# Weight sums by transfers that add in place, a changed order of the seven products, and transposes dealt out between matmuls

## The chip, the cores and the metric

The kernel runs on one core of a Trainium2 chip. The time is device microseconds of one execution; the time given for a kernel is the median of its runs. Engines are named as in the profile: PE (TensorE), DVE (VectorE), ACT (ScalarE), POOL (GpSimd), SP (the queue that issues most transfers).

## The reference, cut to what matters

Two layers work on x of 1024 rows by 1024 columns. Layer 0 mixes rows by differential attention, layer 1 by retention. Each layer norms its input, applies a scale and shift, projects, mixes, projects out and adds the normed result:

```python
h = rms_norm(x) * (1 + scale) + shift          # per layer
q, k, v, g = split(einsum("bsd,de->bse", h, w_in))   # layer 1: widths 1024, 1024, 2048, 2048
y = silu(g) * head_rms_norm(mix(q, k, v))      # layer 1: retention, 4 heads, 256 and 512 wide
x = x + gate * rms_norm(einsum("bse,ed->bsd", y, w_out))
```

What the change touches is the step from layer 0 to layer 1 and layer 1's product h·w_in, with h 1024x1024 and w_in 1024x6144, both f32.

## The kernel before

**Precision.** Matmuls take f16. Each f32 operand is split into a high and a low f16 part, and three matmuls (high·high, high·low, low·high) stand for one f32 product. The split of a weight tile is `prepare`: an ACT copy (L810, high part) and a DVE operation (L811, low part).

**Layer 1's input products.** The 6144 columns of w_in are taken as 12 blocks (`Columns`; per head c_q for q and k, c_v for v, c_g for the gate), each of two groups of 256 columns. A block of w_in has four quarters B11, B12, B21, B22 of 512x256 f32 (512 KB), and h has quarters too (A11 and so on, and their differences S1, M2, N3, N4). A block is computed with seven products of quarters instead of eight, listed with the chain (a PSUM bank) that each is added to:

```python
PRODUCTS = (("x", "A11", "B11"), ("y", "A12", "B21"), ("x", "M2", "T2"), ("z", "S1", "T1"),
            ("x", "N3", "T3"), ("x", "A22", "T4"), ("z", "N4", "B22"))
```

The sums are T1 = B11 + B12, T3 = B12 + B22, T2 = B22 + T1, T4 = B21 + T2. In `prepare` they are four DVE additions per block (L798), three ahead of the split of T2 and one ahead of T4. T2 takes B22's buffer, so B22 is loaded a second time for the last product: five loads of 512 KB per block, all issued by SP (L773). Raw quarters have 4 buffers (`raws1`), split weights 5 (`ws1`); a product's weight is prepared three products ahead (`AHEAD`) and loaded further ahead (`LOADS`).

`product` (L837) runs the matmuls of one product: 256 columns each for q and k, for which h is the moving operand or the weight by column group, and 512 columns for v and g. It then copies a chain's value aside on ACT (L851), or adds kept values on DVE (L846). A chain that starts anew needs a PSUM bank whose former value has been read.

**The turn from layer 0 to layer 1.** Row tiles of 128 rows leave layer 0 by `out0(t)`: the out-projection (`outproj`, 48 matmuls of 512 columns, L574), its norm and the residual (`residual`, L586 on ACT, L589 and L591 on DVE), the store of x, and the norm of the next layer (L304 on ACT, L146 and L149 on POOL, L629 on DVE), which gives `xns[t]`. `out0_hT(j)` turns row tiles 2j and 2j+1 into the quarters of h: 16 transposes of 128x128 f32 on PE in 4 groups of 4 (L651), after each group two scaled copies on ACT (L653) that empty its PSUM bank, and after two groups the sums and splits of h's quarters (L658 to L668 on DVE and ACT). The order of these steps is a string that ends in `... o5 y7 o6 h2 o7`: the 16 transposes of pair 2 stand between the projections of row tiles 6 and 7. The 16 transposes of pair 3 stand in the first block of layer 1, in one piece, after product 2 of the second group of rows (`(n, m) == (2, 1)`); the other half of that block (g = 1) needs them.

**What sets the order.** From `o6` on, PE runs in the order in which the code is written; the other engines' order is set by a scheduler when the kernel is built. Every engine works through its own queue in order: an instruction that waits holds all behind it. At the very end, 16 tiles of the last out-projection's weight (`wo1`) are put where older tiles come free; tile 3 takes a buffer of v ("vr").

Of the kernel before, what the change touches and what calls it, by code (L numbers as in the profile page):

```python
# [20 lines left out]
F16 = mybir.dt.float16  # L21
# [5 lines left out]
P = 128  # L27
# [60 lines left out]
def trunk(ctx: ExitStack, tc: tile.TileContext, a: dict, out: bass.AP):  # L88
# [476 lines left out]
            nc.vector.scalar_tensor_tensor(out=y[t][:, e], in0=o[:, i * P : (i + 1) * P], scalar=f[:, i : i + 1], in1=y[t][:, e], op0=ALU.mult, op1=ALU.mult)  # L565


    def outproj(yT, wo):
        res = []
        for n in range(2):  # L570
            ps = mm()
            for k in range(NK):
                for yi, wi in ((0, 0), (0, 1), (1, 0)):
                    nc.tensor.matmul(  # L574
                        ps, yT(yi, k), wo[k // 4][:, k % 4, wi, n * 512 : (n + 1) * 512],
                        start=(k == 0 and yi == 0 and wi == 0), stop=(k == NK - 1 and yi == 1),
                    )
            res.append(ps)
        return res
# [40 lines left out]
    def out0(t):  # L620

        xt = xres[t // 2][:, t % 2, :]
        ps = outproj(yTs[t], wts["o"])
        x1 = ys.tile([P, D], F32, name="x1", tag=f"y{t}")
        _, add = residual(ps, x1, gps[0], xt, xt)
        add(slice(0, D))
        nc.gpsimd.dma_start(out=x1_d[:, t, :], in_=xt)
        r = row_rsqrt(xt, D, 1.0, NORM_EPS)
        nc.vector.tensor_scalar(out=x1, in0=xt, scalar1=r, scalar2=None, op0=ALU.mult)  # L629
        xns[t] = x1  # L630

    def out0_hT(j):

        if j == 0:
            hA.extend(big.tile([P, 2, 2, 2, 512], F16, name="hA", tag="sb", bufs=3) for _ in range(2))
            hB.append(big.tile([P, 4, 2, 512], F16, name="hB", tag="sb", bufs=3))
            hS.extend(hts.tile([P, 2, 2, 2, 512], F16, name="hS", tag=f"h{k}") for k in range(4))
        n = slice(j * P, (j + 1) * P)
        for kh in range(2):

            pa, ta, ba = (early, "qs", 2) if j == 0 else (ys, f"y{2 * j - 2 + kh}", 1)
            pb, tb, bb = (early, "ks", 2) if j < 2 else (ys, f"y{2 * j - 4 + kh}", 1)
            t = pa.tile([P, 4, 2, P], F32, name="hq", tag=ta, bufs=ba)
            t2 = pb.tile([P, 4, 2, P], F32, name="hq2", tag=tb, bufs=bb)
            for i in range(2):
                ps = sc()
                for kk in range(2):
                    k = 2 * kh + kk + 4 * i
                    for b in range(2):
                        c = (2 * kk + b) * P  # L650
                        nc.tensor.transpose(out=ps[:, c : c + P], in_=xns[2 * j + b][:, k * P : (k + 1) * P], identity=ident)  # L651
                    m = mods[1, k]
                    nc.scalar.activation(  # L653
                        out=t[:, 2 * i : 2 * i + 2, kk], in_=ps[:, 2 * kk * P : 2 * (kk + 1) * P].rearrange("p (b e) -> p b e", b=2),
                        func=AF.Identity, scale=m[:, 1:2], bias=m[:, 0:1],
                    )
            for i in range(2):
                nc.vector.tensor_tensor(out=t2[:, i], in0=t[:, 1], in1=t[:, 3 * i], op=ALU.subtract)  # L658
            nc.vector.tensor_tensor(out=t2[:, 2], in0=t[:, 0], in1=t2[:, 1], op=ALU.subtract)
            nc.vector.tensor_tensor(out=t2[:, 3], in0=t[:, 2], in1=t2[:, 2], op=ALU.subtract)  # L660
            for src, dst, sign in (
                (t[:, 0:4:3], lambda b: hA[kh][:, :, :, b, n].rearrange("p a k e -> p (a k) e"), -1.0),
                (t[:, 2], lambda b: hB[0][:, 2 * kh : 2 * kh + 2, b, n], 1.0),
                (t2[:, 0:2].rearrange("p a k e -> p (a k) e"), lambda b: hS[2 * kh][:, :, :, b, n].rearrange("p a k e -> p (a k) e"), 1.0),
                (t2[:, 2:4].rearrange("p a k e -> p (a k) e"), lambda b: hS[2 * kh + 1][:, :, :, b, n].rearrange("p a k e -> p (a k) e"), 1.0),
            ):
                nc.scalar.activation(out=dst(0), in_=src, func=AF.Copy, scale=sign)
                nc.vector.scalar_tensor_tensor(out=dst(1), in0=src, scalar=sign, in1=dst(0), op0=ALU.mult, op1=ALU.subtract)  # L668

    def load_wo():  # L670
        wts["o"] = load_wout(a["da_w_out"][0], gsub)
# [51 lines left out]
    for h in range(6):  # L723
# [13 lines left out]
        "f": lambda t: flush(),  # L737
        "y": out0_yT,
        "o": out0,
        "h": out0_hT,  # L740
    }
    order = (
        "a0 q1 q2 a1 q0 a2 q3 b0 b1 v5 b2 v4 a3 b3 f0 y0 y1 v7 y2 v6 a4 b4 a5 y3 w0 o0 "
        "o1 b5 a6 a7 b6 y4 o2 b7 f0 y5 o3 h0 o4 y6 h1 o5 y7 o6 h2 o7"
    )
    for c in order.split():
        if c == "o6":
# [22 lines left out]
    def raw_block(src):  # L770
# [4 lines left out]


    PRODUCTS = (
        ("x", "A11", "B11"), ("y", "A12", "B21"), ("x", "M2", "T2"), ("z", "S1", "T1"),
        ("x", "N3", "T3"), ("x", "A22", "T4"), ("z", "N4", "B22"),
    )  # L780

    class Columns:
# [6 lines left out]

        def load(self, n):  # L790

            for b in {0: ("B11",), 1: ("B21", "B12"), 2: ("B22",)}.get(n, ()):
                self.raw[b] = raw_block(self.src(int(b[1]) - 1, int(b[2]) - 1))

        def prepare(self, n):

            r = self.raw
            add = lambda o, x: nc.vector.tensor_tensor(out=r[o], in0=r[o], in1=r[x], op=ALU.add)  # L798
            name = PRODUCTS[n][2]
            if name == "T2":  # L800
                add("B11", "B12")
                add("B12", "B22")
                add("B22", "B11")
                r["T1"], r["T3"], r["T2"] = r["B11"], r["B12"], r["B22"]
            elif name == "T4":
                add("B21", "T2")
                r["T4"] = r["B21"]
                r["B22"] = raw_block(self.src(1, 1))
            w = self.place[n]() if n in self.place else ws1.tile([P, 4, 2, 256], F16, name="w1", tag="w1")
            nc.scalar.activation(out=w[:, :, 0, :], in_=r[name], func=AF.Copy, scale=SW)  # L810
            nc.vector.scalar_tensor_tensor(out=w[:, :, 1, :], in0=r[name], scalar=SW, in1=w[:, :, 0, :], op0=ALU.mult, op1=ALU.subtract)  # L811
            self.w[n] = w

    class Quarters:
# [10 lines left out]
        def product(self, n, new):  # L825
# [20 lines left out]
                nc.vector.tensor_tensor(out=dst, in0=shape(src), in1=dst, op=op)  # L846
                return dst

            if n in (0, 2, 4):
                self.kept[n] = self.hold(n)  # L850
                nc.scalar.activation(out=self.kept[n][0], in_=self.kept[n][1](src), func=AF.Copy)  # L851
            if n == 1:
                self.done("11", add(0, src, ALU.subtract), 1.0)
            elif n == 4:
                self.done("22", add(4, self.acc["z"][:, 0:width], ALU.add), 1.0)
            elif n == 5:
                self.done("21", src, -1.0)
            elif n == 6:
                self.done("12", add(2, src, ALU.add), 1.0)

    def bank_for(u):
        return lambda chain: mm() if chain == "x" or u == 0 else tr()
# [19 lines left out]
    def four_tiles(cols, u, c):  # L882

        parts = [(slice(i * 256, (i + 1) * 256), None, slice((2 * u + i) * P, (2 * u + i + 1) * P)) for i in range(2)]
        two = lambda x: x.rearrange("p (b e) -> p b e", b=2)
        at = lambda q: c[:, (q[0] == "2") : 4 : 2, (q[1] == "2") * 256 : (q[1] == "2") * 256 + 256]

        def done(q, src, sign):
            if q == "21":
                nc.scalar.activation(out=at(q), in_=two(src), func=AF.Copy, scale=sign)  # L890

        return Quarters(cols, parts, lambda n: (at({0: "11", 2: "12", 4: "22"}[n]), two), done)

    steps1 = []

    def retain(h):

# [12 lines left out]
        if h == 0:  # L910
            for g in range(2):
                us = {}
                for n in range(7):
                    for m in range(2):
                        def step(n=n, m=m, g=g, us=us):
                            if n == 0 and m == 0 and g == 0:
                                begin()
                            if n == 0:
                                us[m] = queries_keys(h, st["qT"], st["kT"], c_q, m, slice(g * 256, (g + 1) * 256))
                            us[m].product(n, bank_for(m))  # L920
                            if g == 0 and (n, m) == (2, 1):
                                out0_hT(3)
                        steps1.append((c_q, n, step))
        else:
            us = {}
# [182 lines left out]

    wanted = list(dict.fromkeys((cols, n) for cols, n, _ in steps1))
    AHEAD, LOADS = 3, 6  # L1110
    ready = loaded = 0
    for cols, n, step in steps1:
        at = wanted.index((cols, n))
        while ready < min(at + AHEAD + 1, len(wanted)):
            while loaded < min(ready + LOADS - AHEAD, len(wanted)):
                wanted[loaded][0].load(wanted[loaded][1])
                loaded += 1
            wanted[ready][0].prepare(wanted[ready][1])
            ready += 1
        step()  # L1120


    w_out1 = a["ret_w_out"][0]
    wo1 = {}
    for n in range(2):
        for h in range(RET_HEADS):
# [1 line left out]
            if i < 3:  # L1128
                t = big.tile([P, 4, 2, 512], F16, name="wo1", tag="sb", bufs=3)
            elif i == 3:  # L1130
                t = ret2().tile([P, 4, 2, 512], F16, name="wo1", tag="vr", bufs=2)
            else:
                t = hts.tile([P, 4, 2, 512], F16, name="wo1", tag=f"h{i - 4}")
            for j in range(2):
# [88 lines left out]
```

## Time and profile before

| | |
|---|---|
| median of 3 runs | 1379.69 us (1378.15 to 1382.76) |
| the profiled execution's own time | 1381.89 us |
| its span | 1379.8 us |
| mean granted PE clock | 0.987 |
| stages by the trace | layer 0 to about 640 us, layer 1's blocks to about 1200 us, last projection to the end |

The profile is one execution. A median of busy shares hides the stages, so the trace is read by stretches: busy time of each engine, and the clock that PE was granted as a share of full speed.

### The profile page before, as it was taken

Reading aid. Unit: us, or ns where it says so; the run is one execution under the profiler, and the core shown is the slowest. Engines: PE = TensorE matmul, PEld = TensorE weight load, DVE = VectorE, ACT = ScalarE, POOL = GpSimd, SP = SyncE. Lnnn points to the kernel's source line nnn. Section 1 sums busy time; section 2 is a strip of 40 time slices with the busy share of each in tenths; the row PEclk is TensorE's granted clock in tenths of the full one; section 3 lists DMA queues with packets and bytes.
Section 4 is the critical chain, followed back from the end, with each engine's and each line's share of the span. In section 5 each row is a group of like instructions: output and inputs, shape, how many; then the busy total and the mean of one; then the engine's idle time right before and its main releaser. Section 6 shows DMA issues by size and latency. Waiting matters only on the chain.

```text
span 1379.8 us, 21360 instructions
## 1 busy us (share of the span) xinstructions
PE 1291.8 (94%) x8285; PEld 775.2 (56%) x8285; DVE 948.4 (69%) x1830; ACT 669.3 (49%) x1298; POOL 146.7 (11%) x254
## 2 busy tenths in 40 slices
PE   3899999999999998878999999999999999989998
PEld 2444455455445544435886658765876586634443
DVE  4866996997887786695559865986598658742011
ACT  4854544654555565565445644564456445621000
POOL 2000110111101121221001200120011001100000
PEclk9999999999999999988999999999999999999999
DMA  9723544566352356542321234233323443365330
GB/s 299 242 79 71 133 103 100 144 153 138 100 141 56 89 122 157 136 133 93 75 79 62 94 100 107 62 102 93 106 62 95 116 115 108 73 179 130 92 92 31
DMA packets 249462, 153.94 MB, mean 112 GB/s; under 512 B 147864, under 2 KB 238160, under 8 KB 249360
## 3 DMA queue, kind: packets, MB, share of 16 engines
q1 hardware_dynamic: 246192, 141.29, 39.2%
q0 software_dynamic: 3168, 11.28, 2.6%
q8 instruction: 65, 1.06, 0.3%
q14 instruction: 37, 0.30, 0.1%
HBM read 102.21 MB, written 14.68 MB: 85 GB/s over the span
## 4 chain that ended last, share of the span: by engine, by line
PE 42%; DVE 5%; ACT 5%; DMA 2%; POOL 1%; issue 1%; SPq 0%; POOLq 0%; DVEq 0%; ACTq 0%
PE ps_mm L837 20%; PE ps_av L1170 6%; PE ps_mm L1170 5%; PE ps_tr L837 5%; PE ps_sc L1019 2%; PE ps_av L1042 1%; PE ps_av L1049 1%; DMA raw1o<-in_ret_w_out 1%; PE ps_mm L574 1%; DMA raw<-in_ada_w 1%; ACT junk L304 1%; ACT sg L1060 1%; POOL rs L149 1%; POOL rs L146 1%; DVE w L811 1%
## 5 line engine op out<-in xcount | busy, mean ns | idle before, releaser
L343 PE MATMUL ps_mm<-w,hT 128*128 128x512 f16 x768 | 176.6, 380 | 0.0
L837 PEld LDWEIGHTS <-hS 128*128 128x128 f16 x1536 | 149.6, 98 | 20.5
L331 PE MATMUL ps_mm<-hT,w 128*128 128x512 f16 x624 | 142.2, 379 | 0.0
L811 DVE SCALAR_TENSOR_TENSOR w<-raw,w 128x1024 f16<-128x1024 f32 x82 | 99.9, 1220 | 56.8 <-ACT w L810 56.8
L837 PE MATMUL ps_mm<-w,hS 128*128 128x256 f16 x1152 | 131.6, 273 | 0.0
L523 ACT ACTIVATE sb<-sb,mx 128x128 f32<-128x128 f32 (+7 forms) x128 | 98.2, 768 | 65.2 <-DVE mx L516 64.7
L343 PEld LDWEIGHTS <-hT 128*128 128x128 f16 x768 | 74.5, 98 | 82.9 <-issue 0.8
L810 ACT ACTIVATE w<-raw 128x1024 f16<-128x1024 f32 x82 | 85.8, 1049 | 53.9 <-issue 33.7
L837 PEld LDWEIGHTS <-w 128*128 128x128 f16 x744 | 73.7, 99 | 64.5 <-issue 1.6
L516 DVE CUSTOM_DVE_ANT_0 sb<-ps_sc,table 128x512 f32<-128x512 f32 (+3 forms) x128 | 73.3, 585 | 36.5 <-PE ps_sc L513 28.7
L331 PEld LDWEIGHTS <-w 128*128 128x128 f16 x624 | 60.1, 98 | 67.4
L574 PE MATMUL ps_mm<-w_o,yT 128*128 128x512 f16 x384 | 92.7, 389 | 0.0
L837 PE MATMUL ps_mm<-w,hA 128*128 128x256 f16 x768 | 87.8, 273 | 0.0
L837 PEld LDWEIGHTS <-hA 128*128 128x128 f16 x768 | 74.8, 98 | 10.0
L1170 PEld LDWEIGHTS <-yT 128*128 128x128 f16 x480 | 46.9, 98 | 56.7
L178 DVE SCALAR_TENSOR_TENSOR acc<-raw,cond,acc 128x256 f32<-128x256 f32 x140 | 65.6, 480 | 10.7 <-DMA raw<-in_ada_w 9.2
L534 ACT ACTIVATE sb<-sb 128x896 f16<-128x896 f32 (+6 forms) x64 | 43.3, 678 | 55.4 <-DVE sb L531 55.3
L546 PEld LDWEIGHTS <-dT 128*128 128x128 f16 x864 | 53.7, 99 | 28.5 <-DMA dT<-sb 20.1
L512 PE MATMUL ps_sc<-ks,qs 128*128 128x512 f16 (+3 forms) x192 | 62.1, 330 | 6.9 <-DVE mx L516 6.7
L837 PE MATMUL ps_mm<-hS,w 128*128 128x512 f16 (+1 forms) x336 | 63.3, 346 | 0.0
L513 PE MATMUL ps_sc<-kl,qs 128*128 128x512 f16 (+3 forms) x192 | 62.0, 329 | 0.0
L574 PEld LDWEIGHTS <-yT 128*128 128x128 f16 x384 | 38.1, 100 | 41.8 <-issue 3.8
(205 smaller groups left out, 2290.9 us busy)
## 6 DMA issues: line engine op xcount, KB each, us to landing
raw<-in_ret_w_in SPq DMA_DIRECT2D x60, 512.0 KB, 3.7
raw<-in_ada_w SPq DMA_DIRECT2D x40, 512.0 KB, 6.4
raw<-in_da_w_in SPq DMA_DIRECT2D x16, 1024.0 KB, 6.0
raw1o<-in_ret_w_out SPq DMA_DIRECT2D x16, 512.0 KB, 4.6
y_d<-y SPq DMA_DIRECT2D x24, 256.0 KB, 2.2
x<-in_x SPq DMA_DIRECT2D x8, 512.0 KB, 7.6
raw<-in_ada_w SPq DMA_DIRECT2D x4, 1024.0 KB, 5.3
raw_o<-in_da_w_out SPq DMA_DIRECT2D x4, 1024.0 KB, 5.0
```

The source lines that it names most:

```text
L178: nc.vector.scalar_tensor_tensor(out=acc, in0=parts[k], scalar=cond[:, k : k + 1], in1=acc, op0=ALU.mult, op1=ALU.add)
L331: nc.tensor.matmul(ps, w[:, k, wi, lo : lo + P], hT[k][g][:, xi, :], start=(k == 0 and wi == 0 and xi == 0), stop=(k == NK - 1 and wi == 1),)
L343: nc.tensor.matmul(ps, hT[k][g][:, xi, j * P : (j + 1) * P], w[:, k, wi, :], start=(k == 0 and wi == 0 and xi == 0), stop=(k == NK - 1 and ...
L512: nc.tensor.matmul(ps[c][:, 0:n], qs[:, c, q], ks[:, c, k], start=True, stop=False)
L513: nc.tensor.matmul(ps[c][:, 0:n], qs[:, c, q], kl[c][:, k], start=False, stop=True)
L516: nc.vector.tensor_tensor_reduce(out=sb[:, c, k], in0=ps[c][:, 0:n], in1=table[:, S - L + lo : S - L + lo + n], scale=-es, scalar=(3.0e38 ...
L523: nc.scalar.activation(out=sb[:, c, 0:L], in_=sb[:, c, 0:L], func=AF.Exp, scale=-1.0, bias=mx[:, m0 + c : m0 + c + 1], accum_out=z[:, 4 * ...
L574: nc.tensor.matmul(ps, yT(yi, k), wo[k // 4][:, k % 4, wi, n * 512 : (n + 1) * 512], start=(k == 0 and yi == 0 and wi == 0), stop=(k == NK ...
L810: nc.scalar.activation(out=w[:, :, 0, :], in_=r[name], func=AF.Copy, scale=SW)
L811: nc.vector.scalar_tensor_tensor(out=w[:, :, 1, :], in0=r[name], scalar=SW, in1=w[:, :, 0, :], op0=ALU.mult, op1=ALU.subtract)
L837: nc.tensor.matmul(ps[:, pc], l, r, start=(first and i == 0 and k == 0 and wi == 0 and xi == 0), stop=(k == 3 and wi == 1), skip_group_che ...
L1170: nc.tensor.matmul(pso[t, n], yT1[t][2 * (k // 8) + yi][:, k % 8, :], wo1[k // 4, n][:, k % 4, wi, :], start=(k == 0 and yi == 0 and wi == ...
```

## The change

**Sums.** The four DVE additions per block (48 in all) go. In their place POOL issues four transfers per block that add to what lies in the destination: B11 += B12 and B12 += B22, both with the source in DRAM, give T1 and T3 in place; T1 += B22 from the loaded tile gives T2 in T1's own buffer; B21 += T2 gives T4. They are written in a new function `sums`, called one product ahead of `prepare`. B22 keeps its own buffer, so its second load goes: 4 loads by SP in place of 5.

**Order of products.** T2 now overwrites T1, so the product with T1 (chain z) comes third and that with T2 (chain x) fourth. B22 is loaded with product 3, and the value kept from product 2 is kept from product 3.

**Transposes.** `out0_hT` becomes a generator that stops after each group of four transposes. `h2` goes from the order; during `o7`, four transposes of pair 2 stand ahead of every 12 matmuls. Those of pair 3 are dealt out four at a time after steps (2,1), (3,0), (3,1) and (4,0) of the first half block.

**A buffer.** Tile 3 of the last weight takes the buffer "kN" of the pool `ret` instead of "vr".

```diff
...
-    def outproj(yT, wo):
+    def outproj(yT, wo, between=iter(())):
...
             for k in range(NK):
+                if k % 4 == 0:
+                    next(between, None)
                 for yi, wi in ((0, 0), (0, 1), (1, 0)):
...
-        ps = outproj(yTs[t], wts["o"])
+        ps = outproj(yTs[t], wts["o"], out0_hT(2) if t == 7 else iter(()))
...
+                if i == 0:
+                    yield
...
+            yield
...
-        "o1 b5 a6 a7 b6 y4 o2 b7 f0 y5 o3 h0 o4 y6 h1 o5 y7 o6 h2 o7"
+        "o1 b5 a6 a7 b6 y4 o2 b7 f0 y5 o3 h0 o4 y6 h1 o5 y7 o6 o7"
...
-        ("x", "A11", "B11"), ("y", "A12", "B21"), ("x", "M2", "T2"), ("z", "S1", "T1"),
+        ("x", "A11", "B11"), ("y", "A12", "B21"), ("z", "S1", "T1"), ("x", "M2", "T2"),
...
-            for b in {0: ("B11",), 1: ("B21", "B12"), 2: ("B22",)}.get(n, ()):
+            for b in {0: ("B11",), 1: ("B21", "B12"), 3: ("B22",)}.get(n, ()):
...
+        def sums(self, n):
+
+            r = self.raw
+            add = lambda o, x: nc.gpsimd.dma_start(out=r[o], in_=x, accum_op=ALU.add)
+            rows = lambda i, j: self.src(i, j).rearrange("(k p) e -> p k e", p=P)
+            if n == 2:
+                add("B11", rows(0, 1))
+                add("B12", rows(1, 1))
+                r["T1"] = r["T2"] = r["B11"]
+                r["T3"] = r["B12"]
+            elif n == 3:
+                add("T2", r["B22"])
+            elif n == 5:
+                add("B21", r["T2"])
+                r["T4"] = r["B21"]
+
         def prepare(self, n):
...
-            add = lambda o, x: nc.vector.tensor_tensor(out=r[o], in0=r[o], in1=r[x], op=ALU.add)
...
-            if name == "T2":
-                add("B11", "B12")
-                add("B12", "B22")
-                add("B22", "B11")
-                r["T1"], r["T3"], r["T2"] = r["B11"], r["B12"], r["B22"]
-            elif name == "T4":
-                add("B21", "T2")
-                r["T4"] = r["B21"]
-                r["B22"] = raw_block(self.src(1, 1))
...
-            if n in (0, 2, 4):
+            if n in (0, 3, 4):
...
-                            if g == 0 and (n, m) == (2, 1):
-                                out0_hT(3)
+                            if g == 0 and (n, m) >= (2, 1):
+                                if not last_hT:
+                                    last_hT.append(out0_hT(3))
+                                next(last_hT[0], None)
...
+            while summed <= ready:
+                wanted[summed][0].sums(wanted[summed][1])
+                summed += 1
             wanted[ready][0].prepare(wanted[ready][1])
             ready += 1
         step()
+        while summed < min(at + AHEAD + 2, loaded):
+            wanted[summed][0].sums(wanted[summed][1])
+            summed += 1
...
-                t = ret2().tile([P, 4, 2, 512], F16, name="wo1", tag="vr", bufs=2)
+                t = ret.tile([P, 4, 2, 512], F16, name="wo1", tag="kN", bufs=1)
...
```

**PE between row tiles 6 and 7.** These are PE's rows at the last matmuls of `o6` and the first transposes of pair 2 (`ps_sc` is the bank of a group, `x1` the normed row tiles 4 and 5), before:

```order
L574 LDWEIGHTS yT_5811
L574 MATMUL ps_mm_5968<-w_o_5056,yT_5811 128x512
L651 MATMUL ps_sc_6012<-ident_90,x1_5789 128x128
L651 MATMUL ps_sc_6012<-ident_90,x1_5919 128x128
L651 MATMUL ps_sc_6012<-ident_90,x1_5789 128x128
L651 MATMUL ps_sc_6012<-ident_90,x1_5919 128x128
L651 MATMUL ps_sc_6019<-ident_90,x1_5789 128x128
```

and of the change, where a group of four is followed by matmuls of row tile 7:

```order
L576 LDWEIGHTS yT_5811
L576 MATMUL ps_mm_5968<-w_o_5056,yT_5811 128x512
L653 MATMUL ps_sc_6013<-ident_90,x1_5789 128x128
L653 MATMUL ps_sc_6013<-ident_90,x1_5919 128x128
L653 MATMUL ps_sc_6013<-ident_90,x1_5789 128x128
L653 MATMUL ps_sc_6013<-ident_90,x1_5919 128x128
L576 LDWEIGHTS yT_5939
L576 MATMUL ps_mm_6010<-w_o_5047,yT_5939 128x512
```

The second group now comes 12 matmuls (24 rows with their weight loads) behind the first, in another bank.

**ACT in the same stretch.** The names are raw buffers of the first block: in the kernel before, raw1_6152 is T2 (in B22's buffer), 6146 is T1, 6150 is T3; `hq` are the scaled copies that empty a group of transposes. Before:

```order
L810 ACTIVATE w1_6163<-raw1_6152 128x4x256
L810 ACTIVATE w1_6166<-raw1_6146 128x4x256
L586 ACTIVATE junk_117,ss_5994<-ps_mm_5968 128x512
L653 ACTIVATE hq_6010<-ps_sc_6012,mod1_0_1426 128x2x128
L810 ACTIVATE w1_6203<-raw1_6150 128x4x256
L653 ACTIVATE hq_6010<-ps_sc_6012,mod1_1_1684 128x2x128
L653 ACTIVATE hq_6010<-ps_sc_6019,mod1_4_2689 128x2x128
L653 ACTIVATE hq_6010<-ps_sc_6019,mod1_5_2947 128x2x128
```

and in the change, where 6146 is first T1, then T2:

```order
L821 ACTIVATE w1_6162<-raw1_6146 128x4x256
L588 ACTIVATE junk_117,ss_5994<-ps_mm_5968 128x512
L655 ACTIVATE hq_6011<-ps_sc_6013,mod1_0_1426 128x2x128
L655 ACTIVATE hq_6011<-ps_sc_6013,mod1_1_1684 128x2x128
L821 ACTIVATE w1_6166<-raw1_6146 128x4x256
L304 ACTIVATE junk_117,ss_6004<-xres_5806 128x1024
L655 ACTIVATE hq_6011<-ps_sc_6032,mod1_4_2689 128x2x128
L821 ACTIVATE w1_6203<-raw1_6150 128x4x256
L655 ACTIVATE hq_6011<-ps_sc_6032,mod1_5_2947 128x2x128
```

T1's split comes first and T2's behind the first group's copies; each now stands in the queue ahead of copies of a later group.

**POOL in the same stretch.** `rs` are norm factors of row tiles, `x1_d` the store of x; raw1_6155 is B22 and 6148 is B21. Before:

```order
L627 DMA x1_d_101<-xres_5393 128x1024
L146 TENSOR_SCALAR rs_5932<-ss_5930 128x1
L149 TENSOR_TENSOR rs_5932<-rs_5932,negh_99 128x1
L148 TENSOR_SCALAR rs_5999<-ss_5994 128x1
L149 TENSOR_TENSOR rs_5999<-rs_5999,negh_99 128x1
L627 DMA x1_d_101<-xres_5806 128x1024
```

and in the change:

```order
L629 DMA x1_d_101<-xres_5393 128x1024
L146 TENSOR_SCALAR rs_5932<-ss_5930 128x1
L803 DMA raw1_6146<-in_ret_w_in 128x4x256
L149 TENSOR_TENSOR rs_5932<-rs_5932,negh_99 128x1
L803 DMA raw1_6146<-raw1_6155 128x1024
L148 TENSOR_SCALAR rs_5999<-ss_5994 128x1
L149 TENSOR_TENSOR rs_5999<-rs_5999,negh_99 128x1
L803 DMA raw1_6148<-raw1_6146 128x1024
L629 DMA x1_d_101<-xres_5806 128x1024
```

Three adding transfers have come between the norm factors and the stores of the last row tiles.

## Rows read from the trace of the kernel before

**Rows 1.** The page's first part: busy time, share of the span, instructions.

```profile
PE 1291.8 (94%) x8285; PEld 775.2 (56%) x8285; DVE 948.4 (69%) x1830; ACT 669.3 (49%) x1298; POOL 146.7 (11%) x254
```

**Rows 2.** Windows by stage: window, length, busy time and count by engine, clock, DMA share, GB/s.

```profile
core 0: us, PE busy (x) PEld busy (x) DVE busy (x) ACT busy (x) POOL busy (x), PEclk, DMA share, GB/s
...
600.00:700.00 100.00, 86.26 (x622) 63.75 (x620) 63.52 (x100) 49.20 (x96) 10.48 (x18) 0.90 0.33 94
700.00:1200.00 500.00, 491.96 (x3660) 351.03 (x3658) 372.54 (x522) 256.34 (x416) 44.70 (x67) 1.00 0.31 90
```

**Rows 3.** Windows of the turn, and of one later half block.

```profile
600.00:611.40 11.40, 11.40 (x55) 5.22 (x53) 10.30 (x14) 5.05 (x9) 3.05 (x5) 1.00 0.36 93
611.40:623.20 11.80, 4.08 (x17) 2.63 (x16) 10.83 (x15) 9.71 (x18) 3.20 (x5) 0.60 0.54 177
623.20:635.60 12.40, 12.40 (x50) 5.23 (x48) 5.07 (x11) 3.33 (x7) 0.00 (x0) 0.83 0.00 1
635.60:643.50 7.90, 7.90 (x74) 6.99 (x72) 4.22 (x6) 4.45 (x11) 4.23 (x8) 1.00 0.43 158
643.50:651.50 8.00, 3.38 (x20) 2.20 (x18) 6.22 (x13) 6.38 (x13) 0.00 (x0) 0.78 0.50 160
651.50:663.60 12.10, 12.10 (x98) 10.26 (x97) 6.56 (x16) 5.43 (x12) 0.00 (x0) 0.87 0.01 1
...
786.20:822.40 36.20, 36.20 (x169) 16.43 (x168) 26.34 (x33) 17.22 (x27) 2.38 (x4) 1.00 0.36 113
```

**Rows 4.** Waits in 600 to 660 us: engine, line, releaser: total, times, longest.

```profile
PE ps_sc L651 <- ACT hq L653: 12.3, 8, 3.6
```

**Rows 5.** Timeline of the turn: start, length, engine, line, operation [idle before, releaser].

```profile
604.19 2.35 DVE L811 SCALAR_TENSOR_TENSOR w<-raw,w 128x1024 f16<-128x1024 f32 x2
...
605.62 1.01 POOL L146 TENSOR_SCALAR rs<-ss 128x1 f32<-128x1 f32 x1 [0.43 <-ACT junk L304]
...
612.23 2.00 ACT L810 ACTIVATE w<-raw 128x1024 f16<-128x1024 f32 x2 [5.12 <-DVE raw L798]
...
615.31 1.12 PE L651 MATMUL ps_sc<-ident,x 128*128 128x128 f32 x4 [3.61 <-ACT hq L653]
...
619.33 1.05 ACT L304 ACTIVATE junk<-xres 128x1024 f16<-128x1024 f32 x1
...
622.77 0.69 PE L651 MATMUL ps_sc<-ident,x 128*128 128x128 f32 x2 [2.69 <-ACT hq L653]
...
641.25 0.75 DVE L629 TENSOR_SCALAR x<-xres,rs 128x1024 f32<-128x1024 f32 x1 [2.24 <-POOL rs L149]
...
645.12 0.66 PE L651 MATMUL ps_sc<-ident,x 128*128 128x128 f32 x4 [1.18 <-ACT hq L653]
```

**Rows 6.** Groups by line over the whole span: busy time, mean ns, idle before.

```profile
L811 DVE SCALAR_TENSOR_TENSOR w<-raw,w 128x1024 f16<-128x1024 f32 x82 | 99.9, 1220 | 56.8 <-ACT w L810 56.8
...
L810 ACT ACTIVATE w<-raw 128x1024 f16<-128x1024 f32 x82 | 85.8, 1049 | 53.9 <-issue 33.7 <-PE ps_tr L837 12.1 <-DVE raw L798 7.0
...
L798 DVE TENSOR_TENSOR raw<-raw,raw 128x1024 f32<-128x1024 f32 x48 | 58.7, 1222 | 1.1
...
L653 ACT ACTIVATE hq<-ps_sc,mod 128x256 f32<-128x256 f32 x32 | 16.9, 560 | 4.2 <-PE ps_sc L651 3.9
...
L627 POOL DMA_DIRECT2D x_d<-xres x8 | 4.9, 616 | 15.4 <-DVE xres L591 15.2 <-issue 0.2
```

**Rows 7.** DMA issues: operation, count, KB each, median us from issue to landing.

```profile
raw<-in_ret_w_in SPq DMA_DIRECT2D x60, 512.0 KB, 3.7
...
x_d<-xres POOLq DMA_DIRECT2D x8, 512.0 KB, 3.7
...
gp<-in_post_gain POOLq DMA_DIRECT2D x2, 512.0 KB, 4.7
```

**Rows 8.** Timeline: two evictions of product chains and what waits for one.

```profile
674.29 1.47 PE L837 MATMUL ps_tr<-hS,w 128*128 128x256 f16 x12 [1.40 <-DVE held L846]
...
691.62 0.68 DVE L846 TENSOR_TENSOR sg<-ps_mm,sg 128x512 f32<-128x512 f32 x1
```

**Rows 9.** PE's waits in 960 to 1220 us.

```profile
PE ps_sc L1019 <- DVE a L1002: 2.7, 3, 1.9
...
PE ps_mm L1170 <- DVE wo L1141: 1.7, 2, 1.5
```

More of the change, by code (lines that the diff above doesn't have):

```diff
@@ L739, in trunk @@
         "o": out0,
-        "h": out0_hT,
+        "h": lambda j: list(out0_hT(j)),
     }
@@ L858, in product @@
             elif n == 6:
-                self.done("12", add(2, src, ALU.add), 1.0)
+                self.done("12", add(3, src, ALU.add), 1.0)
     def bank_for(u):
@@ L890, in done @@
                 nc.scalar.activation(out=at(q), in_=two(src), func=AF.Copy, scale=sign)
-        return Quarters(cols, parts, lambda n: (at({0: "11", 2: "12", 4: "22"}[n]), two), done)
+        return Quarters(cols, parts, lambda n: (at({0: "11", 3: "12", 4: "22"}[n]), two), done)
     steps1 = []
+    last_hT = []
     def retain(h):
@@ L1110, in trunk @@
     AHEAD, LOADS = 3, 6
-    ready = loaded = 0
+    ready = loaded = summed = 0
     for cols, n, step in steps1:
```

## The prediction

> **What bounds the kernel now.** I read the page's first part, then busy time by stage, then the stage with the most idle PE finely: its windows, PE's waits, the timeline. PE is busy 94% of the span and DVE 69% [rows 1], but the stages differ. From 700 to 1200 us PE works 491.96 of 500 us at clock 1.00 [rows 2]: all idle time there is 8.0 us, so the DVE additions inside it (48 in the kernel, 58.7 us together [rows 6]) are hidden, and taking them away gives next to nothing. The room is in the turn between the layers: from 600 to 700 us PE works 86.26 us, and the granted clock is 0.90 [rows 2].
>
> The turn's windows show two holes. In 611.4 to 623.2 PE works 4.08 of 11.8 us at 0.60; the 48 matmuls of row tile 7 behind it take 12.4 us at 0.83. In 643.5 to 651.5 it works 3.38 of 8.0 us at 0.78, and the next 12.1 us run at 0.87 [rows 3]. Both holes are the 16 transposes of a pair in one piece: PE waits for ACT to empty the banks with L653, 8 waits, 12.3 us [rows 4]. The reader should see how: four transposes take 0.66 us undisturbed, and the waits ahead of them are 3.61 us (behind ACT's splits of T2 and T1, which waited 5.12 us for DVE's additions), 2.69 and 1.18 us [rows 5].
>
> **What a transfer that adds costs.** The trace has none, and this is the main unknown; call D its time from issue to landing. Below: a plain transfer of the same 512 KB lands 3.7 us after its issue, from SP's queue and from POOL's; the slowest median of that size on POOL's queue is 4.7 [rows 7]. An add reads two operands and writes one; if it moves at half the speed throughout, D is twice 3.7, 7.4, at the far end twice 4.7, 9.4. I take 5.6, midway between 3.7 and 7.4, since only the moving part of the 3.7 should double, and keep 3.7 and 9.4 for the range. Writing out a plain 512 KB store takes POOL 0.62 us [rows 6]; for 1 KB rows, of which there are four times as many, I allow 1.2 (an estimate). The Trainium skill ("Collectives: The Full Stack", Part 3, "Why 7× under link rate") says that the add inside a transfer costs nothing by itself, but the second source read goes through the same ring and halves the rate. That is at most 7.4 here; no run so far shows it.
>
> **The first hole, with D.** B11's add can be issued when its two splits are done and POOL has written the norm factor ahead of it: DVE's splits of B11 and B21 run from 604.19 for 2.35 us, POOL's L146 from 605.62 for 1.01 us [rows 5], so 606.6. T1 lands at 606.6 + D; its splits (1.05 on ACT, 1.22 on DVE [rows 6]) and a semaphore's 0.1 let T2's add start at 609.0 + D, which lands at 609.0 + 2D. ACT's queue now has T2's split behind the first group's copies and ahead of the norm's square (L304) and the second group's copies, so ACT stands still until then. Behind it lie 1.05 (T2), 1.25 (L304, 1.05 + 0.2), 0.56, 1.05 (T3) and 0.56 [rows 5, 6]: the second group's bank is empty at 613.5 + 2D, and the fourth group of transposes can start 0.3 later (the sets of four transposes use two banks). By PE's own work the fourth group is due at 611.3 + 3 x (0.7 + 2.6) = 621.2 (12 matmuls of 512 columns at full clock take 2.6, a quarter of some 10.4). With D = 5.6 it starts at 625.0 instead, 3.8 late; adding its 0.7, the last 2.6 and 1.5 for stretches at less than full clock, row tile 7's projection ends at 629.8 instead of 635.6 [rows 3]: **-5.7 us**.
>
> **The second hole.** The normed row tile 7 was ready 6.4 us after its projection's end (635.60 by the window, L629 from 641.25 for 0.75 [rows 3, 5]). In the change the splits of the last group of pair 2 and of T4 fall into that stretch, and I allow two splits on ACT and 0.5 for them (2.6 us): ready at 629.8 + 9.0 = 638.8. The 7.9 us of products ahead of the first group [rows 3] end at 637.7, so PE waits 1.1, and the first four transposes start near 639 instead of 643.5 (-4.5). From there to the second half of the block lie 16 transposes (4 x 0.7), the remaining eight products (12.1 us at clock 0.87 [rows 3], so 10.5 at full clock), and 2.3 that I allow for waits between the groups (twice the wait of 1.18 [rows 5]): 15.6 us instead of 20.1 (8.0 and 12.1 [rows 3]), another **-4.5**. The second half starts at 654.6 instead of 663.6: **-9.0** with the first hole's gain in it.
>
> **Behind the turn.** In the first v block T1's split waits for its add's landing (+1.5) and T2's (+1.0) while the 1.40 us wait of 674.29 [rows 8], which stood behind DVE's additions, goes: +1.1. For the later 10 blocks: a half block of v or g takes some 36 us [rows 3], T1's add is issued a product ahead, and its buffer's use lies over two products behind; T2's landing has room up to D of some 9 to 11. ACT stands still D - 3 us per block, with nothing due soon behind it. POOL is busy 44.70 of 500 us [rows 2]; four adds a block put some 4 us on it and hold norm factors of the heads by up to D; those are needed a tile later.
>
> Chain y is now followed at once by z, which may want y's bank. An eviction starts 0.2 to 0.3 us after its product and takes 0.68 [rows 8]; where DVE is busy with other work, 1 us is lost now and then, **+1** in all. Against it, DVE has 58.7 us less [rows 6], of which PE's waits for DVE in the later blocks can profit: 2.7 us for L1002 in 960 to 1220 us [rows 9] and as much again in the blocks before, of which I count **-3**. The last weight tile's new buffer comes free earlier: PE waits 1.7 us for it [rows 9]; **-1**. The SP loads that go (12 of 512 KB) lie in a stage with a DMA share of 0.31 [rows 2] and give nothing.
>
> The sum: -9.0 + 1.1 + 1 - 3 - 1 = -10.9 us against the profiled execution's 1381.9, so 1371.0; its own time lies 2.2 above the runs' median, so the median becomes 1369.
>
> **Rivals.** *Waits on ACT eat the gain.* From D = 5.6 on, each us of D costs 4: two in the first hole, where two adds follow each other, and two in the first v block. If D is 7.4, 7.2 of the 10.9 go: profile 1378, median 1376. For it speaks that nothing in the trace shows an add; against it, that the 3.7 holds a start that should not double. *Adds too slow: slower than before.* The sum is zero at D = 8.3. At D = 9.4 the turn gives 15.2 back, and from about D = 9 on each of 11 later blocks loses time where T2 is late, some 0.3 each: +7, median 1387; at D = 12, with 1.2 us for each block, about 1408. A way to it is that POOL writes a transfer's list of rows slowly while DVE works: the 3.7 and 4.7 of POOL's stores, with DVE busy 69% of the time [rows 1, 7], speak against it. The Trainium skill ("SBUF — State Buffer", the trap headed "DVE blocks DMA") says that transfers issued by POOL can starve while DVE runs an operation in its two-port mode, since their descriptors can't be written; those two landings show no such thing, but neither has 1 KB rows.
>
> *z behind y stalls.* If z waits in each of 12 blocks for y's eviction, 0.7 us each [rows 8], 8.4 go and the median is 1378.
>
> *Adds as quick as plain loads.* D = 3.7: the fourth group starts when it is due, so the first hole gives 5.4 more, the first v block 2.5 more, and row tile 7's matmuls run at full clock (12.4 us at 0.83 [rows 3], so 2.1 less): -21, median 1359. That the change does not do what it says, the holes staying, would need the transposes to wait for something else; the rows of PE and ACT show no other releaser than L653 [rows 4].
>
> **How the numbers follow.** The forecast (D from 4.6 to 6.9) has 0.53, ACT's waits 0.17, slow adds 0.20, z behind y 0.05, quick adds 0.05. The predicted time is the forecast's, 1369, with 1362 to 1376 of its own. The range goes from the value at D = 3.7 to that at 9.4, 1359 to 1387; beyond it lie half of the slow adds and half of the quick ones, and small tails of the rest. A measurement of this kernel can tell about 0.3% (4.1 us) from no change. Faster by more (below 1375.6): the forecast but 0.02, quick adds, and 0.06 of ACT's waits, 0.62. Slower (above 1383.8): slow adds, and 0.01 of ACT's waits, 0.21. The rest, 0.17.
>
> **What would show it.** In the profile after: the landing time of the accumulating transfers (5 to 6.5 us); no transposes in one piece; row tile 7's matmuls between them, at a granted clock over 0.83; L821 of T2 on ACT waiting some 5 us in the first block; the second half of the first block starting near 655; PE's idle time in 700 to 1200 us still about 8 us. The forecast is wrong if the adds land after more than 8 us, if PE waits for splits of T2 or T4 in each block, or if PE's busy time rises.

## The result and the profile after

The changed kernel takes 1395.16 us (median of 4 runs, 1394.05 to 1396.99) against 1380.28: a ratio of 1.0108, 95% interval 1.0087 to 1.013. It is slower by 1%, and the forecast was faster by 0.8%.

The page and the windows by stage (columns as in [rows 2]) after:

```profile
PE 1293.7 (93%) x8285; PEld 774.6 (56%) x8285; DVE 892.5 (64%) x1782; ACT 670.5 (48%) x1298; POOL 193.8 (14%) x302
```

```profile
600.00:700.00 100.00, 83.85 (x621) 61.75 (x620) 54.99 (x94) 48.41 (x95) 18.09 (x26) 0.97 0.53 119
700.00:1200.00 500.00, 482.92 (x3577) 343.26 (x3575) 315.28 (x465) 246.27 (x398) 81.62 (x105) 1.00 0.54 119
```

DVE has 56 us less to do than in [rows 1], and PE's own work is nearly the same. But the stage that had 8.0 us of idle PE [rows 2] now has 17.1. The DMA issues, as in [rows 7]:

```profile
raw<-in_ret_w_in SPq DMA_DIRECT2D x48, 512.0 KB, 4.5
...
raw<-in_ret_w_in POOLq DMA_DIRECT2D x24, 512.0 KB, 6.4
raw<-raw POOLq DMA_DIRECT2D x24, 512.0 KB, 4.6
```

The transfers that add land after 6.4 us (from DRAM, 1 KB rows) and 4.6 us (tile to tile): the mean of the two is 5.5, and the forecast had assumed 5.6 for both. So the main unknown was right in the mean, and the sign of the forecast wrong.

To see where the time went, each trace is cut at three starts: PE's first transpose of pair 2, the first product of the first v block, and the last projection's first matmul that adds a product of `yT` to `ps_av`. "Turn" lies between the first two, "later" between the next two, "end" behind. One profiled execution each, us; the median is that of the runs, and the ratio goes by the runs of the kernel before on the same chip (medians 1379.1 to 1380.8), with its 95% interval. For e2 both leave out one run of 3857.22 us, far above its other three:

| kernel | median | ratio to before | turn | later | end |
|---|---|---|---|---|---|
| before | 1380.28 | | 72.1 | 547.5 | 148.9 |
| changed | 1395.16 | 1.0108 (1.0087-1.0130) | 71.8 | 559.2 | 149.1 |
| e1 transposes dealt out alone | 1374.14 | 0.9965 (0.9951-0.9978) | 67.1 | 546.1 | 148.9 |
| e2 changed, transposes in one piece | 1398.75 | 1.0140 (1.0119-1.0160) | 79.0 | 559.8 | 149.1 |
| e3 changed, sums by DVE | 1381.97 | 1.0014 (1.0002-1.0026) | 69.3 | 548.8 | 149.2 |
| e4 changed, T2 and T4 by DVE | 1381.35 | 1.0010 (0.9997-1.0023) | 68.6 | 549.6 | 149.1 |
| e5 = e1 with the new order | 1381.01 | 1.0006 (0.9997-1.0016) | 73.3 | 546.2 | 148.9 |
| e6 changed, T2 in B22's buffer | 1395.25 | 1.0102 (1.0078-1.0127) | 73.0 | 562.7 | 148.9 |
| e7 changed, T2 by DVE | 1385.25 | 1.0041 (1.0025-1.0058) | 69.0 | 553.7 | 149.1 |
| e8 = e1 with the new buffer | 1374.10 | 0.9963 (0.9951-0.9975) | 66.1 | 546.5 | 148.9 |
| e10 = e1, copies behind four transposes | **1360.97** | 0.9866 (0.9845-0.9887) | 56.5 | 545.6 | 148.9 |
| e11 before, copies behind four transposes | 1366.11 | 0.9896 (0.9875-0.9918) | 60.7 | 547.1 | 150.5 |
| e12 changed, T2 split after T3 | 1385.85 | 1.0041 (1.0026-1.0056) | 72.9 | 550.2 | 149.1 |
| e13 changed, copies behind four transposes | 1387.24 | 1.0054 (1.0038-1.0070) | 63.7 | 562.9 | 149.1 |
| e14 changed, T4 by DVE | 1402.60 | 1.0171 (1.0153-1.0189) | 71.9 | 565.4 | 149.1 |

So the loss lies in "later" (+11.7), and the turn gave 0.3 where 9.0 was forecast. The spans of the two profiles differ by 12.5 us, the medians by 14.9; the profiles account for the 12.5.

**Where "later" loses.** PE's waits after, 700 to 1200 us (columns as in [rows 4]):

```profile
PE ps_sc L1033 <- DVE a L1016: 12.2, 14, 2.2
PE ps_tr L252 <- DVE sg L857: 3.3, 3, 1.2
PE ps_sc L1033 <- DVE y L980: 1.6, 1, 1.6
```

L1033 is the state's matmul of the retention steps; before, the same matmul (L1019) waited 4.6 us in that stretch:

```profile
PE ps_sc L1019 <- DVE a L1002: 4.4, 6, 1.9
...
PE ps_sc L1019 <- DVE y L966: 0.2, 1, 0.2
```

These waits grew by 9.2 us, most of the 11.7. Part of the rest is clock: behind the longest of them (2.19 us, ended at 1174.30) the granted clock from 1175 to 1185 us is 0.86. The timeline around one of these waits, after:

```profile
853.34 0.88 POOL L803 DMA_DIRECT2D raw<-raw  x1 [9.10 <-DVE w L822]
...
857.87 1.06 ACT L821 ACTIVATE w<-raw 128x1024 f16<-128x1024 f32 x1 [1.79 <-DMA raw<-raw]
...
858.84 0.40 ACT L1017 ACTIVATE aT<-a 128x256 f16<-128x256 f32 x1
...
861.50 0.68 DVE L857 TENSOR_TENSOR sg<-ps_mm,sg 128x512 f32<-128x512 f32 x1
...
862.22 1.91 ACT L970 ACTIVATE vr<-sg 128x2048 f16<-128x2048 f32 x1 [0.96 <-DVE sg L857]
...
864.16 2.29 DVE L971 SCALAR_TENSOR_TENSOR vr<-sg,vr 128x2048 f16<-128x2048 f32 x1 [1.98 <-ACT vr L970]
...
868.95 0.28 DVE L1016 TENSOR_TENSOR a<-ps_sc,dec 128x128 f32<-128x128 f32 x1
...
869.28 1.46 PE L1033 MATMUL ps_sc<-y,kN 128*128 128x512 f16 x6 [0.74 <-DVE a L1016]
```

Read it downwards. T2's add is issued at 853.34; ACT comes to T2's split and stands 1.79 us for the landing. Behind it in ACT's queue waits the copy of the scores (L1017), and so in turn DVE's eviction (L857) and the splits of v; they follow late, and L1016, which empties the scores' bank, ends at 869.23. PE's L1033 needs that bank and waited 0.74 us. Before, the same place of the same head shows no wait:

```profile
856.22 0.42 ACT L1003 ACTIVATE aT<-a 128x256 f16<-128x256 f32 x1 [0.74 <-DVE a L1002]
...
861.78 2.29 DVE L957 SCALAR_TENSOR_TENSOR vr<-sg,vr 128x2048 f16<-128x2048 f32 x1
...
865.54 2.81 PE L1019 MATMUL ps_sc<-y,kN 128*128 128x512 f16 x12
```

DVE's split of v (L957) began 0.81 us ahead of PE's next scores at 862.59 then, and just behind them (864.13) now (L971). That this chain starts with ACT's wait is a reading of one place; e12 and e7 below test it.

**Why the turn gave so little.** From 600 to 700 us PE waits 10.1 us for copies of transposes (12.3 before [rows 4]), but 6.0 us for evictions of products in three places, where it waited 1.4 before [rows 8]. Two of the three, after:

```profile
672.21 1.06 ACT L821 ACTIVATE w<-raw 128x1024 f16<-128x1024 f32 x1 [4.33 <-DMA raw<-in_ret_w_in]
...
673.59 2.78 PE L848 MATMUL ps_mm<-hS,w 128*128 128x256 f16 x24 [1.96 <-ACT held L862]
...
680.89 1.06 ACT L821 ACTIVATE w<-raw 128x1024 f16<-128x1024 f32 x1 [4.04 <-DMA raw<-raw]
...
683.92 5.40 PE L848 MATMUL ps_mm<-w,hA 128*128 128x256 f16 x48 [2.31 <-DVE qT L889]
```

The splits of T1 and T2 of the first v block stand in ACT's queue, 4.33 and 4.04 us long, for their adds to land. Behind them in the queue stand copies of the block in work (L862 and L888), and PE waits for them, the second time by way of DVE's L889.

### The profile page after: what moved, and what is told of

Its sections match the earlier page's. It is cut to its first block, busy times and chain, and to the rows that moved or that the text cites. A ratio compares the mean times of both kernels' runs of the same rounds, so it can differ in the third digit from the quotient of the medians.

```text
span 1392.3 us, 21410 instructions
## 1 busy us (share of the span) xinstructions
PE 1293.7 (93%) x8285; PEld 774.6 (56%) x8285; DVE 892.5 (64%) x1782; ACT 670.5 (48%) x1298; POOL 193.8 (14%) x302
## 4 chain that ended last, share of the span: by engine, by line
PE 29%; DMA 6%; DVE 6%; ACT 4%; issue 3%; SPq 2%; POOL 2%; POOLq 0%; DVEq 0%; ACTq 0%
PE ps_mm L848 13%; PE ps_av L1190 5%; PE ps_mm L1190 5%; DMA raw<-in_ret_w_in 3%; PE ps_tr L848 2%; DMA raw<-raw 2%; SPq L956 1%; PE ps_sc L1033 1%; DVE w L822 1%; PE ps_av L1063 1%; DMA raw1o<-in_ret_w_out 1%; PE ps_av L1056 1%; DVE sg L857 1%; ACT sg L1074 1%; DVE y L1069 1%
## 5 line engine op out<-in xcount | busy, mean ns | idle before, releaser
L516 DVE CUSTOM_DVE_ANT_0 sb<-ps_sc,table 128x512 f32<-128x512 f32 (+3 forms) x128 | 73.3, 585 | 36.3 <-PE ps_sc L513 30.0
L848 PEld LDWEIGHTS <-hA 128*128 128x128 f16 x768 | 74.8, 98 | 12.5 <-issue 2.5
```

Source lines behind the costliest of these rows:

```text
L516: nc.vector.tensor_tensor_reduce(out=sb[:, c, k], in0=ps[c][:, 0:n], in1=table[:, S - L + lo : S - L + lo + n], scale=-es, scalar=(3.0e38 ...
L848: nc.tensor.matmul(ps[:, pc], l, r, start=(first and i == 0 and k == 0 and wi == 0 and xi == 0), stop=(k == 3 and wi == 1), skip_group_che ...
```

## The experiments

Theory W: the adds hold ACT's (and POOL's) queue, and what stands behind is late; dealing out gains. Rival O: the new order of products costs. Rival D: dealing out brings nothing.

**e1, dealing out alone.** The kernel before with the diff's parts on `out0_hT`, `outproj` and `last_hT`, nothing else.

> The kernel before with only the transposes dealt out (pairs 2 and 3); sums by DVE, old order of products, old buffer. Theory W (the loss comes from waits for the adding transfers: ACT's split of T2 and POOL's norm factors hold what stands behind them, and the dealing out itself gains): about 1372, since both holes of the turn shrink and nothing else changes. Rival D (dealing out brings nothing, because ACT's copies are as late between matmuls): 1379 to 1382. Rival O (the loss comes from the new order of products and what the scheduler makes of it): about 1372 too.

1374.14. D falls. PE's rows in its turn show how little idle time that took away:

```profile
613.37 0.69 PE L653 MATMUL ps_sc<-ident,x 128*128 128x128 f32 x2 [3.61 <-ACT hq L655]
613.86 5.30 PE L576 MATMUL ps_mm<-w_o,yT 128*128 128x512 f16 x12
...
620.03 0.44 PE L653 MATMUL ps_sc<-ident,x 128*128 128x128 f32 x2 [0.66 <-ACT hq L655]
620.31 2.75 PE L576 MATMUL ps_mm<-w_o,yT 128*128 128x512 f16 x12
```

All eight waits are still there (10.5 us instead of 12.3), each between the second and third transpose of a group. What is gained beside them is clock: after a wait of 3.61 us twelve matmuls take 5.30 us, after one of 0.66 us 2.75. In the whole turn PE's idle time fell by 1.9 us, and its busy time, for the same work, by 3.2.

**e2, the rest without dealing out.** `h2` and `out0_hT(3)` back in one piece.

> The changed kernel with the transposes in one piece again, as before (sums by transfer, new order, new buffer stay). W: 1399 to 1403, the 1395 plus what dealing out gains. D: 1395, no change. O: as W.

1398.75: dealing out is worth some 4 us in the changed kernel too (3.6 between the medians, 4.4 by the ratios, whose intervals overlap; turn 79.0 against 71.8, later alike).

**e3 and e4, who adds.** e3: all four sums by DVE, in place, with B22 loaded one product earlier; e4: only T2 and T4. The edit of e3 in part:

```diff
-            add = lambda o, x: nc.gpsimd.dma_start(out=r[o], in_=x, accum_op=ALU.add)
+            add = lambda o, x: nc.vector.tensor_tensor(out=r[o], in0=r[o], in1=x, op=ALU.add)
```

> The changed kernel with the four sums of a block made in place by DVE again, from loaded quarters; order of products, four loads per block, dealt transposes and buffer stay. W: at most 1374, since no split and no norm factor waits for a transfer any more, and PE's waits in the retention steps (L1033, 13.8 us in the changed kernel, 4.4 before) go back to some 5. O: 1388 to 1395, those waits stay. D: about 1385.

> The changed kernel with T1 and T3 still by adding transfers from DRAM, but T2 and T4 (whose operands are tiles in use) by DVE. W: 1374 to 1380, since the waits of ACT for the tile-to-tile adds (20.1 us) go and those for the others (5.5 us) stay, as do the issues in POOL's queue. O: 1388 to 1395.

1381.97 and 1381.35, both above the ranges of W and below those of O. With the adds from DRAM the time is the same as without any; the tile-to-tile adds cost 14 us. But 7 to 8 us above e1 remain, so O holds in part.

**e5, the order alone**, on e1, with the old sums.

```diff
-        ("x", "A11", "B11"), ("y", "A12", "B21"), ("x", "M2", "T2"), ("z", "S1", "T1"),
+        ("x", "A11", "B11"), ("y", "A12", "B21"), ("z", "S1", "T1"), ("x", "M2", "T2"),
```

> The kernel with only the transposes dealt out (1374), plus the new order of products alone: DVE's sums stay as they were before (T2 in B22's buffer, B22 loaded twice), moved ahead of T1's split. If the order itself costs the 8 us by which in-place DVE sums with the new order stood above that kernel: 1380 to 1383, with the longer waits behind DVE's evictions (2.3 us instead of 1.2 at the end of a head). If they came from making T2 in place, behind T1's splits: about 1374.

1381.01: the order, with these sums ahead of T1's split, costs 7 us against e1 (6 by the ratios). The place is not that of the expectation: "later" is unchanged (546.2), the turn is 6.2 longer. Its PE waits, 600 to 700 us:

```profile
PE ps_sc L653 <- ACT hq L655: 9.8, 8, 3.7
PE ps_tr L842 <- DVE held L851: 3.7, 1, 3.7
PE ps_mm L842 <- DVE held L851: 1.7, 1, 1.7
```

e1 has 1.4 us in place of the last two rows' 5.4. In layer 1's first block a product is 12 matmuls of 256 columns, so z comes to y's bank soon; DVE's eviction that it needs (L851, at 669.33) stood behind three additions and a split of the next block's weights, 1.22 us each. The rest is clock (0.93 from 600 to 700 us, 0.97 in e1). The changed kernel has none of these additions; its waits at this place are the 6.0 us shown above. In the later blocks products are longer, and no such wait is seen.

**e6 and e7, T2's add.** e6 makes T2 in B22's buffer (`add("B22", r["T1"])`, B22 loaded again), so that its add doesn't wait for T1's splits; e7 makes T2 alone by DVE.

> The changed kernel with T2 made by transfer in B22's buffer instead of T1's (B22 is loaded a second time, as before), so that its add need not wait for T1's splits. W with the serial chain as cause (T1's splits, then the add, then T2's split): 1382 to 1387, and ACT's splits wait for tile-to-tile adds under 8 us in all instead of 20.1. If the transfers themselves cost (their landing, POOL's queue), whatever they wait for: 1392 to 1397.

> The changed kernel with T2 alone made by DVE, in place; T1, T3 and T4 stay transfers. If T2's add is what ACT and PE wait for: 1381 to 1384, as with T2 and T4 by DVE. If T4's add or POOL's queue costs as much: 1387 to 1391.

1395.25 and 1385.25, the second between its two ranges. Without the wait for T1's splits ACT's waits moved, and the time stayed: those for tile-to-tile adds fell by half, those for adds from DRAM rose. So e6 doesn't show what that wait costs by itself. ACT's waits for adds from 640 us on, e6:

```profile
ACT w L824 <- DMA raw<-in_ret_w_in: 27.9, 7, 5.8
ACT w L824 <- DMA raw<-raw: 10.0, 4, 3.2
```

and the changed kernel:

```profile
ACT w L821 <- DMA raw<-raw: 20.1, 8, 4.0
ACT w L821 <- DMA raw<-in_ret_w_in: 5.5, 2, 4.3
```

**e8, the buffer**, on e1.

> The kernel with only the transposes dealt out, plus the last weight's tile 3 in the other buffer. The prediction's step gave it 1 us. The changed kernel still shows PE's wait of 1.5 us for that weight, so nothing is expected: 1374, within 1.5 us.

1374.10: nothing.

**e9, all splits later.** `AHEAD` 2 for splits, adds where they were. In it T1's split reads what T2's add has already written, so T1's weight isn't T1 and the waits are others.

> The changed kernel with every weight split written two products ahead instead of three, while loads and adding transfers stay where they are, so each add has a product more (2.6 us or 5.4) before the split that waits for it. If what costs is ACT standing still at the split for the landing (W, whatever the add itself waited for): ACT's waits for adds fall from 25.6 to under 10 us and the time to 1383 to 1388. If the adds cost by POOL's queue, by traffic or by the scheduler's order on DVE: 1392 to 1398.

1397.66, with 29.1 us of ACT's waits for tile-to-tile adds: it decides nothing. e12 gives T2's add more time in another way.

**e12, T2's split behind T3's**, in the changed kernel.

```diff
+    prep = []
+    for i in range(0, len(wanted), 7):
+        prep += [wanted[i + j] for j in (0, 1, 2, 4, 3, 5, 6)]
...
-            wanted[ready][0].prepare(wanted[ready][1])
+            prep[ready][0].prepare(prep[ready][1])
```

> The changed kernel with the split of T3 written ahead of that of T2, so that T2's add has one product more before ACT comes to the split that waits for it (its issue and all else stay). If ACT's standing still for that landing is the cause: ACT's waits for tile-to-tile adds fall from 20.1 to some 5 us, time 1383 to 1388. If the adds cost otherwise (POOL's queue, their order on DVE): 1392 to 1398.

1385.85, 9.3 us back with every transfer still there, as expected. ACT's and PE's waits (640 to 1215, and 700 to 1200 us):

```profile
ACT w L821 <- DMA raw<-in_ret_w_in: 4.0, 1, 4.0
ACT w L821 <- DMA raw<-raw: 3.8, 1, 3.8
```

```profile
PE ps_sc L1033 <- DVE a L1016: 5.4, 8, 1.9
```

PE's waits at L1033 fell from 13.8 to 5.4, and "later" from 559.2 to 550.2: the wait of ACT is the cause of these 9 us. The two waits of ACT that are left (672.78 and 681.50) are those of the first v block, in the turn, which stayed as long (72.9). What DVE waits for POOL's norm factors fell little (35.0 to 30.9, 23.0 before).

**e10, e11 and e13, the waits within a group.**

```diff
                         nc.tensor.transpose(out=ps[:, c : c + P], in_=xns[2 * j + b][:, k * P : (k + 1) * P], identity=ident)
-                    m = mods[1, k]
+                for kk in range(2):
+                    m = mods[1, 2 * kh + kk + 4 * i]
                     nc.scalar.activation(
```

> The kernel with only the transposes dealt out (1374), with the two copies of a group written behind its four transposes, not each behind its two. The eight waits that are left there lie between the second and the third transpose of a group (0.7 to 3.6 us, 10.5 us in all). If the third waits because the bank's first half is being read: those waits go, and 1364 to 1368. If PE would be held by the banks anyway (two banks, the copies as late as before): 1371 to 1374.

> The kernel before with that one edit (four transposes, then the two copies), transposes in one piece as before. If the eight waits (12.3 us) are those within the groups: the holes shrink, but two banks for four groups in one piece still make PE wait for copies from the third group on, so 1371 to 1376. If the banks are what holds PE: no change, 1379.

> The changed kernel with the two copies of a group behind its four transposes. That edit took 13 us from the kernel with transposes alone. If the adds cost only in the later blocks: 1382. If ACT's standing still in the turn holds the banks: 1386 to 1390, with PE still waiting for copies there.

On e1 it gives 1360.97, the fastest kernel here and below the expected range. PE's timeline:

```profile
608.09 0.60 PE L653 MATMUL ps_sc<-ident,x 128*128 128x128 f32 x4
608.53 2.75 PE L576 MATMUL ps_mm<-w_o,yT 128*128 128x512 f16 x12
611.12 0.60 PE L653 MATMUL ps_sc<-ident,x 128*128 128x128 f32 x4
611.55 2.75 PE L576 MATMUL ps_mm<-w_o,yT 128*128 128x512 f16 x12
```

No transpose waits for a copy any more, and the clock in 600 to 700 us is 1.00. Alone, on the kernel before, the edit gives 1366.11, although PE still waits 5.4 us for copies in three places: 14.7 us, more than the whole change set out to bring and more than was expected of it. In the changed kernel it brings 8 us, not 13, within the second of the two ranges: there PE still waits 1.8 us for a transpose's copy, and "later" (562.9) keeps its loss.

**e14, T4 by DVE**, T2 by transfer.

> The changed kernel with T4 alone made by DVE; T1, T2 and T3 stay transfers. With T2 alone by DVE it was 1385, with both 1381. If the two add up: 1391. If either of them holds the queues as long: 1385.

1402.60, worse than either expectation: now DVE stands for T2's landing as well (DVE's waits, from 640 us on):

```profile
DVE raw L813 <- DMA raw<-raw: 27.0, 11, 3.9
```

## Why the prediction was wrong, step by step

**D, the landing of an add,** was right in the mean: 5.5 against 5.6. That was luck in part, since neither kind lay there: 4.6 tile to tile and 6.4 from DRAM, beside 4.5 for a plain load of the same kernel. That the moving part doubles isn't shown. The Trainium skill ("Collectives: The Full Stack", Part 3) says of a collective's add that the second source read halves the rate. The rows show no halving here: the tile-to-tile add took 0.1 us more than a plain load, and the medians of both kinds stayed below 7.4. The Trainium skill ("SBUF — State Buffer", the trap "DVE blocks DMA") warns that transfers issued by POOL starve while DVE works in its two-port mode. Nothing here shows that: DVE was busy 64%, and the 24 tile-to-tile adds landed after 4.5 to 6.6 us; the trace doesn't tell in which mode DVE worked.

**"ACT stands still D - 3 us per block, with nothing due soon behind it"** is the step that failed. The idle time itself was forecast about right: from the second v block on ACT waited 8 times, 17.3 us in all, 2.2 each against 2.6. In the code `sums(n)` stands right ahead of `prepare(n)`, so T2's add has only the one product between the splits of T1 and T2: in the rows above it was issued at 853.34, and its sum was wanted at 856.08 (857.87 less the 1.79 us of waiting). But behind the split stood copies of scores, and behind them DVE's evictions that PE needs, so the wait that was put at nothing cost most of the +11.7 us in "later", where -3 was forecast. e12 and e7 show it: with T2's add given one product more, or made by DVE, 9 to 10 us return.

**"In the first v block T1's split waits ... and T2's"**, +1.1 in all, is the same step in the turn, and was too small: PE waited 2.0 and 2.3 us there. The second is gone in e4 and e7, where DVE makes T2.

**"Both holes are the 16 transposes of a pair in one piece"** misread [rows 5]. A row "x4" there joins the last two transposes of one group with the first two of the next, so the wait ahead of it is within a group. The two copies of a group do not both come after its four transposes: the code puts the first behind two of them, and the third transpose then waits for this copy, which reads the bank's first half. Dealing out therefore left all eight waits, and brought 5.0 us (e1) instead of 9.0, most of it clock. In the changed kernel T2's split began at 620.78, as forecast (620.2), but the fourth group only at 630.57 instead of 625.0, behind the wait of 3.26 us within the first group and twelve matmuls at half clock.

**Chain z behind y** was given 1 us and cost 6 to 7 in e5, all in the first block, whose products are shortest; the rival had spread 8.4 over 12 blocks. In e5 the eviction stood behind DVE's additions; what the order costs in the changed kernel, which has none, no run parts from the adds. **The buffer** was given 1 us and brought none (e8). **The DVE sums are hidden** was right: with half of them gone and one wait of ACT in their place (e4) "later" is 549.6, with all of them (e3) 548.8.

**The rival that came true**, slower, had another way there: not slow adds, but adds as quick as forecast behind which an engine waits in order. The sum, from the table: turn -0.3, later +11.7, end +0.3, and 0.8 ahead of the turn, where nothing was changed: 12.5, the difference of the spans.

**Open**: e7 differs from e4 in T4's add alone and takes 4 us more, though ACT waits for no add from the second v block on and DVE's waits for POOL's norm factors are the same (29.0 us). By what way T4's add costs them, no run shows; e14 could not part it from T2's. How much of the cost is the traffic (DMA share 0.54 instead of 0.31) was not tested.

## What to carry to other kernels

An engine that works in order and comes to an instruction before its transfer has landed delays all that stands behind it: list that queue's next entries and who waits for each, and don't judge the wait by the idle time alone. Before moving a wait elsewhere, look at its two neighbours in the unmerged timeline: here the copies' place in four lines of code was worth 20 us together with the dealing out, and the large change lost 15. Work taken from an engine that isn't the bound gave no time back (e4 has half of DVE's additions and takes as long as e3).

## What the runs showed of the hardware

An add by transfer of 512 KB landed after 4.6 us tile to tile in 4 KB rows and after 6.4 us from DRAM in 1 KB rows, a plain load of such a quarter after 4.5 us in the same kernel (3.7 before). To issue one kept POOL for 0.89 us (24, tile to tile) and 1.44 us (24, from DRAM) in the mean. PE's clock: after waits of 3.26 and 3.61 us twelve matmuls of 512 columns took 5.30 us at a granted clock of 0.50, after waits of 0.66 to 1.66 us 2.75 us at 1.00. In the changed kernel:

```profile
615.73 0.69 PE L653 MATMUL ps_sc<-ident,x 128*128 128x128 f32 x2 [3.26 <-ACT hq L655]
616.21 5.30 PE L576 MATMUL ps_mm<-w_o,yT 128*128 128x512 f16 x12
...
623.38 0.44 PE L653 MATMUL ps_sc<-ident,x 128*128 128x128 f32 x2 [1.66 <-ACT hq L655]
623.66 2.75 PE L576 MATMUL ps_mm<-w_o,yT 128*128 128x512 f16 x12
```
